# Full attention begun at the tenth projection step, weight loads in pieces and their squares one group ahead

## The chip, the cores and the metric

The kernel runs on one core of one Trainium2 chip. The metric is device time in microseconds (us), the median of several runs. The engines have short names here: PE (TensorE, matrix products), ACT (ScalarE, activations), DVE (VectorE), POOL (GpSimd), SP (the queue that issues most DMAs).

## What is computed

One layer of a bidirectional encoder over 1024 tokens of width 1024, batch 1, float32. Two groups of heads read one combined projection of the normalised input.

```python
h = _rmsnorm(x, norm_gain[l])
proj = h @ w_in[l]                                  # 1024 x 3328 columns
q_a, k_a, v_a, g_a, q_b, k_b, v_b, g_b = jnp.split(proj, split_at, axis=-1)
q_a = rotary(_rmsnorm(q_a, q_norm_a)); k_a = rotary(_rmsnorm(k_a, k_norm_a))
o_a = _gqa_blocked(q_a, k_a, v_a) * silu(g_a)       # 8 query heads, 2 key heads, full attention
o_b = _neighbourhood_attn(q_b, k_b, v_b, na_rpb) * silu(g_b)   # 8 heads, window 8 x 16 of the token grid
x = x + jnp.concatenate([o_a, o_b], -1) @ w_out[l]
return _rmsnorm(x, final_norm_gain)
```

## The kernel before

Every float32 operand is split into a float16 high part and a float16 remainder, and each product is three matmuls (high x high, high x low, low x high). The 1024 tokens are eight tiles of 128. The weights come as 17 groups of 256 columns, 1 MB each: 0 is keys and values of the full attention (KVA), 1 and 2 its queries (QA), 3 and 4 the queries, 5 and 6 the keys, 7 and 8 the values of the neighbourhood attention (QB, KB, VB), 9 and 10 its gate, 11 and 12 the gate of the full attention, 13 to 16 the output projection. A projection of a group is four "pairs" of two token tiles, 48 matmuls of 128x256 each.

A group's weights are prepared before use. `load_w(g)` has POOL issue the DMA into one of two buffers `raw`. `prep_a` (L281) squares the whole group on ACT and sums by row; the output of the squares, which nobody reads, goes into the group's own future buffer `whl`, of which there are two. `prep_b` sums over the partitions with one small matmul (L293), then DVE (L294) and POOL's power (L295) make the scale. `prep_c` (L300) casts the high part on ACT in two halves, `prep_d` (L307) forms the remainder on DVE. `prep(g)` is called when group g-1 begins and sets the slots of these steps; `PREP` holds delays for single groups; `load_w(g + 2)` comes after the casts.

The order is made in two ways. PE's instructions run in the order in which the program writes them. ACT, DVE, POOL and SP are, after a short opening, ordered by the framework's planner from its own simulated times, with the program's order as the priority. The program itself is written by a small class, `Flow`: it counts slots; `at(delay, position, function)` puts work into a later slot; `queue` holds generators whose every `yield` stands for six projection matmuls (three of 128x512 for KB); `step(n)` runs one slot and then takes n yields from the queue.

First come 12 steps of 8 yields (`fl.step(PAIR)`): groups 0, 1 and 2, a pair a step. Every pair of keys or queries is normalised and rotated (`norm_rope`, L411 to L429, on ACT, DVE and POOL) and transposed by DMA (L447, L480). Then `run_units` goes through 64 units of full attention, one head of one tile each, the four heads of the first query group for all tiles first. A unit is `a_qk` (scores of 128x1024 into one of two PSUM buffers, L592 to L594; a pass of DVE, L601; two exponentials on ACT, L603 and L604), `a_lo` one slot later (remainder on DVE, L609, and a DMA transpose of the probabilities, L614) and `a_pv` (product with the values, L623 to L625) four slots later. Between units PE takes yields of the queue, groups 3 to 8, at a rate of `FILL_A`: 4.2 for four units, 3.4 for seven, then 2.65.

The same follows for 64 units of the neighbourhood attention (`b_qk`, `b_lo`, `b_pv`, L673 to L705, transposes at L692, values five slots later) with the rates `FILL_B` and `FILL_B_END` and groups 9 to 16 in the queue. `SPLIT_AT` names the unit after which each finished tile of the gated output is normalised, split and transposed (`os_a`, `os_b`, `os_c`, L731 to L748). Groups 13 to 16 are used for tiles 0 to 3 two at a time; `out_row(u)` then does one later tile through all four groups, 16 yields, adds to the input (L772), applies the final norm (L796 to L805) and stores (L806). Row 4 is in the queue with the units; rows 5, 6 and 7 come after the last unit.

Of the kernel before, what the change touches and what calls it, by code (L numbers as in the profile page):

```python
# [16 lines left out]
P = 128  # L17
KC = 8
NU = 8
GC = 256  # L20
NH = 8
D = 64
NX = 4
SKEW_A, SKEW_B = 4, 5
FILL_A = [(4, 4.2), (7, 3.4)]
FILL_A_END = 3
FILL_B = [(12, 3.4), (24, 3), (2, 2.5)]
FILL_B_END = 3
SPLIT_AT = (26, 27, 29, 31, 39, 55, 56)
PREP = {2: 4, 3: 0, 4: 2, 12: 0, 13: 0}  # L30
NEG = -1.0e38
EPS = 1e-6
LN_P = 14.0 * float(np.log(2.0))
# [5 lines left out]
KVA, QA, QB, KB, VB, GA, GB = 0, 1, 3, 5, 7, 11, 9  # L39
# [3 lines left out]
class Flow:  # L43
# [8 lines left out]
    def at(self, delay, pos, fn, *a):  # L52
        self.due.setdefault((self.slot + delay, pos), []).append((fn, a))
# [35 lines left out]
def kernel(ctx: ExitStack, tc: tile.TileContext, x: bass.AP, w: bass.AP, wo: bass.AP,  # L89
# [3 lines left out]
    act, dve, pool, pe, sp = nc.scalar, nc.vector, nc.gpsimd, nc.tensor, nc.sync  # L93
# [9 lines left out]
    fl = Flow()  # L103
    at = fl.at
# [46 lines left out]


    raw, wp, late, x2 = {}, {}, {}, {}

    def load_w(g):
        raw[g] = wraw.tile([P, KC, GC], F32, tag="raw", name=f"raw{g}")
        if g in gate:
            pool.tensor_copy(raw[g][:, 0, :1], xr[gate[g]][:, 1:])
        pool.dma_start(raw[g], w[g] if g < 13 else wo[g - 13])

    xts, gate = [], {}
    ones = area(0, [P], F32)[:1]
# [3 lines left out]
    mh = one.tile([P, NU], F32, name="mh")  # L166
# [25 lines left out]
    S_, RC, EC = 0, 17, 34  # L192
# [5 lines left out]
    def col(i, n=1):  # L198
        return sm[:, i:i + n]
# [68 lines left out]

    wss = {}

    def prep_a(g):
# [7 lines left out]
        wss[g] = tn(f"wss{g}", 1, "ws")  # L279
        if g:  # L280
            act.activation(wp[g][0].bitcast(BF16), raw[g], AF.Square, accum_out=wss[g])  # L281
            return
        late["half"] = tn("wssh", 1, "ws")
        act.activation(wp[g][0][:, :4].bitcast(BF16), raw[g][:, :4], AF.Square, accum_out=late["half"])

    def prep_a2(g):
        dve.tensor_tensor_reduce(out=wp[g][0][:, 4:].bitcast(BF16), in0=raw[g][:, 4:], in1=raw[g][:, 4:], scale=1.0,
                                 scalar=late["half"], op0=OP.mult, op1=OP.add, accum_out=wss[g])

    def prep_b(g):  # L290
        pt = ahead.append(proj_tile(f"wt{g}")) or ahead[-1]
        top = [a.bitcast(BF16)[:, 1:2] for a in (mh[:, :1], wss[g])]
        pe.matmul(pt[:, 0, :1], top[0].to_broadcast([P, P]), top[1], start=True, stop=True)  # L293
        dve.tensor_scalar(wss[g], pt[:, 0, :1], -2.0 ** -27, 1e-30, op0=OP.mult, op1=OP.add)  # L294
        pool.tensor_tensor(col(S_ + g), wss[g], mh[:, :1], op=OP.pow)  # L295

    def prep_c(g):
        for i in range(0, KC, KC // 2):
            s = slice(i, i + KC // 2)
            act.activation(wp[g][0][:, s], raw[g][:, s], AF.Copy, scale=col(S_ + g))  # L300

    def prep_d(g):
        ready.add(g)
        n = KC if g == 0 else KC // 2
        for i in range(0, KC, n):
            s = slice(i, i + n)
            dve.scalar_tensor_tensor(wp[g][1][:, s], raw[g][:, s], col(S_ + g), wp[g][0][:, s], op0=OP.mult, op1=OP.subtract)  # L307
# [8 lines left out]
    ready = set()  # L316

    def prep_e(g):
        dve.reciprocal(col(RC + g), col(S_ + g))
# [13 lines left out]

    pend = []

    def prep(g):
        d = PREP.get(g, 1)
        at(d + 1, "pre", prep_a, g)
        at(d + 2, "mid", pend.append, g)

    def sums_now():

        while pend:
            g = pend.pop(0)
            prep_b(g)
            at(1, "pre", prep_c, g)
            at(1, "post", prep_d, g)
            if g + 2 < 17:
                at(2, "pre", load_w, g + 2)

    def fin_scales():
        for hh in range(2):
# [39 lines left out]
        return hT[a][:, k, u * P:(u + 1) * P]  # L392

    kTa = r6(0, [P, NU, 3, P], F16, "kTa")
    va = r6(1, [P, NU, 2, 2, D], F16, "va")
    qTa = [carve(rq, 8192 * i, [NU, 4, P], F16) for i in range(2)]
    klo1 = carve(rq, 16384, [NU, P], F16)

    def norm_rope(g, up, src, nh, kq, done):
        n = 2 * nh  # L400
        s3 = src.rearrange("p a (h d) -> p a h d", d=D)
        if g == KVA:
            both = slot("both", [P, 2, 2, nh, D], F32)
        else:
            both = w4((0, 1, 8, 9)[up] if g == QA + 1 else 4 + up, [P, 2, 2, nh, D], F32, f"qn{g}_{up}")
        qn, t2 = both[:, 0], both[:, 1]
        sq = t2
# [24 lines left out]
        at(1, "mid", b)  # L432
        at(1, "post", c)
        done(qn)
# [375 lines left out]
    PAIR = 8.0  # L810
# [28 lines left out]
    k, q = [kva_gen(up) for up in UP], group(1, [qa_gen(0, up) for up in UP])  # L839
# [34 lines left out]
    x_lo(7, dve)  # L874
    load_w(3)

    for p in range(11):
        fl.step(PAIR)
    fl.add(*group(3, [qb_gen(0, up) for up in UP]))
    fl.add(*group(4, [qb_gen(1, up) for up in UP]))  # L880
# [57 lines left out]
    def out_row(u):  # L938
        last = ([out_gen([(u, 15), (u, 16)], [(u, 1)])] if u < NU - 1 else
                [out_gen([(u, 15)]), out_gen([(u, 16)], [(u, 1)])])  # L940
        return out_gen([(u, 13), (u, 14)], [(u, 0)]), *last
# [101 lines left out]
```

## Time and profile before

| | |
|---|---|
| median of 3 runs | 609.66 us (609.57 to 610.23) |
| the profiled execution | 611.81 us, its span 610.0 us |
| mean granted PE clock | 0.967 |
| PE busy | 534.4 us, 88% of the span |
| DVE, ACT, POOL busy | 440.6, 394.9, 119.3 us |
| DMA queue 1 (transposes and SP's loads) | 67.7% of 16 engines' span |

Busy time is read by stage, since each stage has another limit: a busy share over the whole span mixes them. The profile names an instruction by its line, its engine and its output and inputs; in the timeline a bracket behind an instruction gives the time that its engine had stood idle before it, and what ended that. A DMA has a time to landing, from its issue to its end. The chain of waits follows the work that ended last, back from the end.

### The profile page before, as it was taken

The page shows a single profiled execution, that of the slowest core. Times are in us where ns is not written, and L with a number is a line of the kernel's source. Part 1 is how long each engine was busy: PE and PEld are TensorE (multiplying, and loading weights), DVE is VectorE, ACT ScalarE, POOL GpSimd, SP SyncE. Part 2 cuts the span into 40 slices and gives each one's busy share as a digit, 9 for nine tenths or more (in the row PEclk, how much of TensorE's full clock was granted, in tenths as well). Part 3 has the DMA queues.
Part 4 walks back from the last instruction along what each step waited for, and adds up shares of the span by engine and source line. Part 5 has one row for each costly group of instructions (what it writes and reads, how often), then busy time and mean ns, then how long its engine had stood idle before and what let it go on. Part 6 is the DMA issues. An engine that isn't in the chain of part 4 may idle for free.

```text
span 610.0 us, 13863 instructions
## 1 busy us (share of the span) xinstructions
PE 534.4 (88%) x5541; PEld 405.4 (66%) x5541; DVE 440.6 (72%) x986; ACT 394.9 (65%) x647; POOL 119.3 (20%) x150
## 2 busy tenths in 40 slices
PE   3587989799988979979888979999999789889794
PEld 1376878577864535547666767877777567668684
DVE  4688676987977948957977847586877866778332
ACT  5552454878859858858667727677689986674210
POOL 2396788410000000000000000110111221112100
PEclk9978999999999979989899999999999898999899
DMA  8989433799999999999799894548486996687422
GB/s 231 225 160 247 96 105 106 136 213 195 204 198 168 197 173 169 206 207 187 155 183 210 155 217 122 118 76 134 103 149 122 172 212 145 134 140 183 95 62 70
DMA packets 245972, 97.26 MB, mean 159 GB/s; under 512 B 236561, under 2 KB 237201, under 8 KB 243986
## 3 DMA queue, kind: packets, MB, share of 16 engines
q1 hardware_dynamic: 242306, 75.66, 67.7%
q0 software_dynamic: 3312, 19.92, 11.6%
q10 hardware_dynamic: 288, 0.79, 0.5%
q8 instruction: 43, 0.70, 0.5%
q14 instruction: 23, 0.19, 0.1%
HBM read 31.33 MB, written 4.19 MB: 58 GB/s over the span
## 4 chain that ended last, share of the span: by engine, by line
PE 44%; DMA 14%; issue 14%; DVE 13%; POOL 6%; ACT 5%; SPq 1%; DVEq 0%; POOLq 0%; ACTq 0%
PE pj L369 14%; PE wt L369 7%; DMA ar<-p 6%; PE po L369 5%; PE kb L369 4%; DMA ar<-ar 4%; PE s L592 3%; PE s L594 2%; POOL nt L417 2%; PE sb L674 2%; DVE whl L307 2%; ACT p L604 2%; DVE p L601 1%; PE sb L673 1%; ACT p L603 1%
## 5 line engine op out<-in xcount | busy, mean ns | idle before, releaser
L369 PEld LDWEIGHTS <-hT 128*128 128x128 f16 x2112 | 205.6, 100 | 68.5 <-issue 15.4
L369 PE MATMUL pj<-whl,hT 128*128 128x256 f16 x1584 | 189.2, 275 | 3.4 <-DMA hT<-xhl 1.8
L601 DVE CUSTOM_DVE_ANT_0 p<-s,sm 128x1024 f32<-128x1024 f32 x64 | 82.0, 1281 | 15.4 <-PE s L594 13.9
L603 ACT ACTIVATE p<-s,nm,sm 128x1024 f16<-128x1024 f32 x43 | 51.8, 1204 | 51.1 <-DMA ar<-p 23.4
L369 PE MATMUL wt<-whl,hT 128*128 128x256 f16 x528 | 68.0, 286 | 14.9 <-ACT whl L300 7.1
L604 ACT ACTIVATE p<-s,nm,sm 128x1024 f32<-128x1024 f32 x64 | 76.8, 1200 | 0.0
L609 DVE TENSOR_TENSOR p<-p,p 128x1024 f16<-128x1024 f32 x43 | 52.8, 1229 | 21.7 <-ACT p L604 21.6
L369 PE MATMUL po<-whl,mA 128*128 128x256 f16 x384 | 65.8, 277 | 0.0
L684 ACT ACTIVATE rq<-ar,mx,sm 128x384 f32<-128x384 f32 (+1 forms) x64 | 43.0, 673 | 28.6 <-DVE mx L683 28.4
L295 POOL TENSOR_TENSOR sm<-wss,mh 128x1 f32<-128x1 f32 x17 | 11.0, 645 | 250.1 <-DVE wss L294 237.4
L369 PEld LDWEIGHTS <-mA 128*128 128x128 f16 x512 | 48.7, 100 | 12.3 <-issue 5.0
L369 PE MATMUL po<-whl,mB 128*128 128x256 f16 x192 | 53.1, 277 | 0.0
L592 PE MATMUL s<-kTa,rq 128*128 128x512 f16 x128 | 39.5, 391 | 14.6 <-ACT p L604 14.6
L623 PE MATMUL pv<-va,ar 128*128 128x64 f16 x384 | 39.3, 194 | 8.7 <-DMA ar<-p 7.4
L307 DVE SCALAR_TENSOR_TENSOR whl<-raw,sm,whl 128x1024 f16<-128x1024 f32 (+1 forms) x33 | 44.8, 1371 | 1.9 <-ACT whl L300 1.9
L685 ACT ACTIVATE ar<-ar,mx,sm 128x384 f16<-128x384 f32 (+1 forms) x64 | 42.9, 674 | 1.1
L623 PEld LDWEIGHTS <-ar 128*128 128x128 f16 x384 | 34.7, 99 | 13.1 <-DMA ar<-p 9.3
L300 ACT ACTIVATE whl<-raw,sm 128x1024 f16<-128x1024 f32 x34 | 37.1, 1138 | 5.0 <-POOL sm L295 4.9
L681 DVE CUSTOM_DVE_ANT_0 ar<-sb,bias 128x384 f32<-128x384 f32 x48 | 26.6, 555 | 18.4 <-PE sb L674 15.4
L625 PE MATMUL pv<-va,ar 128*128 128x64 f16 x384 | 39.3, 194 | 0.0
L624 PE MATMUL pv<-va,ar 128*128 128x64 f16 x384 | 39.3, 194 | 0.0
L690 DVE TENSOR_TENSOR ar<-rq,ar 128x384 f16<-128x384 f32 (+1 forms) x64 | 34.1, 533 | 4.8 <-ACT ar L685 4.8
(196 smaller groups left out, 1069.3 us busy)
## 6 DMA issues: line engine op xcount, KB each, us to landing
raw<-in_w_dram POOLq DMA_DIRECT2D x11, 1024.0 KB, 6.7
raw<-in_wo_dram POOLq DMA_DIRECT2D x4, 1024.0 KB, 5.9
x<-in_x_dram SPq DMA_DIRECT2D x7, 512.0 KB, 6.4
khh<-ar SPq DMA_DIRECT2D x16, 128.0 KB, 3.7
x2b<-in_x_dram POOLq DMA_DIRECT2D x4, 512.0 KB, 5.9
x<-in_x_dram POOLq DMA_DIRECT2D x4, 512.0 KB, 6.8
out_dram<-x2b SPq DMA_DIRECT2D x8, 256.0 KB, 3.0
out_dram<-x SPq DMA_DIRECT2D x7, 256.0 KB, 2.9
```

Of the source, the lines that this page charges most:

```text
L307: dve.scalar_tensor_tensor(wp[g][1][:, s], raw[g][:, s], col(S_ + g), wp[g][0][:, s], op0=OP.mult, op1=OP.subtract)
L369: pe.matmul(*o[0], **o[1])
L592: pe.matmul(s[:, c * 512:(c + 1) * 512], q, kTa[:, 4 * c:4 * c + 4, hh], start=True, stop=False)
L601: dve.tensor_tensor_reduce(out=p32, in0=s, in1=col(SHA).to_broadcast([P, 1024]), scale=col(NSA), scalar=3e38, op0=OP.add, op1=OP.min, accu ...
L603: act.activation(hl[:, 0], s, AF.Exp, bias=nm, scale=col(SCA))
L604: act.activation(p32, s, AF.Exp, bias=nm, scale=col(SCA), accum_out=sums[hh, u][:, h:h + 1])
L609: dve.tensor_tensor(hl[:, 1], p32, hl[:, 0], op=OP.subtract)
L623: pe.matmul(o, pt[:, kt], va[:, kt, hh, 0], start=kt == 0, stop=False)
L624: pe.matmul(o, pt[:, kt], va[:, kt, hh, 1], start=False, stop=False)
L625: pe.matmul(o, pt[:, 8 + kt], va[:, kt, hh, 0], start=False, stop=kt == 7)
L684: act.activation(p32, t, AF.Exp, bias=mx, scale=col(SCB + hh), accum_out=sums["b", u][:, h:h + 1])
L685: act.activation(hl[:, 0], t, AF.Exp, bias=mx, scale=col(SCB + hh))
```

## The change

1. The plain projection steps are 9 instead of 12, so full attention begins at the tenth. The last three pairs of group 2 (24 yields) stay in the queue and go between the units; the later rate of `FILL_A` rises from 2.65 to 3.10 yields a unit. The normalisation of group 2 takes two staging areas in turn instead of four, as two of the old ones belong to the units now.
2. Loads of groups 6 to 16 are issued in four pieces of 256 KB, one a slot.
3. For these groups the squares are taken a group ahead, as four ACT instructions of 128x512 with four sums, into a spare area; `prep_b` adds the four sums with four small matmuls. When group g-1 begins, g's cast and remainder follow at once, half a group in each of two slots.
4. `PREP`: group 2 is prepared one step earlier; 12 and 13 have no delay of their own.
5. `FILL_B` and `FILL_B_END` become 3.35 yields for 40 units and 3.1 after. Rows 5 and 6 join row 4 in the queue; by the rates row 5 is done between the units, and row 6 stands between the last tile's `os_b` and `os_c`. `SPLIT_AT` has the tiles 5 and 6 at units 47 and 55 instead of 55 and 56.

```diff
-FILL_B = [(12, 3.4), (24, 3), (2, 2.5)]
-FILL_B_END = 3
-SPLIT_AT = (26, 27, 29, 31, 39, 55, 56)
-PREP = {2: 4, 3: 0, 4: 2, 12: 0, 13: 0}
+FILL_B = [(40, 3.35)]
+FILL_B_END = 3.1
+SPLIT_AT = (26, 27, 29, 31, 39, 47, 55)
+PREP = {2: 3, 3: 0, 4: 2}
...
-        pool.dma_start(raw[g], w[g] if g < 13 else wo[g - 13])
+        src = w[g] if g < 13 else wo[g - 13]
+        if g < 6:
+            pool.dma_start(raw[g], src)
+            return
+        for i in range(4):
+            k = slice(2 * i, 2 * i + 2)
+            issue = lambda k=k: pool.dma_start(raw[g][:, k], src[:, k])
+            at(i, "pre", issue) if i else issue()
...
+    def prep_q(g, i):
+        junk = (va_more if g < 11 else carve(rq, 17408, [512], BF16)).rearrange("p (k c) -> p k c", c=GC)
+        if i == 0:
+            wss[g] = [t[:, 0:1] for t in [tn(f"wss{g}_{k}", 1, "ws") for k in range(4)]]
+        act.activation(junk, raw[g][:, 2 * i:2 * i + 2], AF.Square, accum_out=wss[g][i])
...
-        pe.matmul(pt[:, 0, :1], top[0].to_broadcast([P, P]), top[1], start=True, stop=True)
-        dve.tensor_scalar(wss[g], pt[:, 0, :1], -2.0 ** -27, 1e-30, op0=OP.mult, op1=OP.add)
-        pool.tensor_tensor(col(S_ + g), wss[g], mh[:, :1], op=OP.pow)
+        n = len(wss[g])
+        for i in range(n):
+            pe.matmul(pt[:, 0, :1], top[0].to_broadcast([P, P]), top[1 + i], start=i == 0, stop=i == n - 1)
+        t = wss[g][0]
+        dve.tensor_scalar(t, pt[:, 0, :1], -2.0 ** -27, 1e-30, op0=OP.mult, op1=OP.add)
+        pool.tensor_tensor(col(S_ + g), t, mh[:, :1], op=OP.pow)
...
+    def squares(g, slots):
+        for i, k in enumerate(slots):
+            at(k, "pre", prep_q, g, i)
+        at(slots[-1], "mid", pend.append, g)
+
     def prep(g):
-        d = PREP.get(g, 1)
-        at(d + 1, "pre", prep_a, g)
-        at(d + 2, "mid", pend.append, g)
+        if g < 6:
+            d = PREP.get(g, 1)
+            at(d + 1, "pre", prep_a, g)
+            at(d + 2, "mid", pend.append, g)
+            if g == 5:
+                squares(g + 1, (7, 7, 8, 8))
+            return
+        at(1, "pre", alloc_wp, g)
+        for i, h in enumerate(HALVES):
+            at(1 + i, "pre", prep_c, g, [h])
+            at(1 + i, "post", prep_d, g, [h])
+        if g + 2 < 17:
+            at(3, "pre", load_w, g + 2)
+        if g < 16:
+            squares(g + 1, (4, 5, 6, 7) if g < 13 else (2, 2, 3, 3))
...
-            both = w4((0, 1, 8, 9)[up] if g == QA + 1 else 4 + up, [P, 2, 2, nh, D], F32, f"qn{g}_{up}")
+            both = w4(8 + up % 2 if g == QA + 1 else 4 + up, [P, 2, 2, nh, D], F32, f"qn{g}_{up}")
...
-    for p in range(11):
+    for p in range(8):
         fl.step(PAIR)
...
-    mid = (6 * 32 - sum(n * r for n, r in FILL_A) - FILL_A_END * SKEW_A) / (64 - n_head) + 0.02
+    mid = (6 * 32 + 24 - sum(n * r for n, r in FILL_A) - FILL_A_END * SKEW_A) / (64 - n_head) + 0.02
...
-    fl.add(*out_row(4))
+    fl.add(*out_row(4), *out_row(5), *out_row(6))
...
-    for u in range(5, NU):
-        fl.add(*out_row(u))
-        while fl.queue:
-            fl.step(PAIR)
+    fl.add(*out_row(7))
+    while fl.queue:
+        fl.step(PAIR)
```

More of the change, by code (lines that the diff above doesn't have):

```diff
@@ L269, with alloc_wp @@
     wss = {}
-    def prep_a(g):
+    def alloc_wp(g):
         if g < 15:
@@ L278, in prep_a @@
         wp[g] = (t[:, 0], t[:, 1])
-        wss[g] = tn(f"wss{g}", 1, "ws")
+    def prep_a(g):
+        alloc_wp(g)
+        wss[g] = [tn(f"wss{g}", 1, "ws")]
         if g:
-            act.activation(wp[g][0].bitcast(BF16), raw[g], AF.Square, accum_out=wss[g])
+            act.activation(wp[g][0].bitcast(BF16), raw[g], AF.Square, accum_out=wss[g][0])
             return
@@ L284, in prep_a @@
         act.activation(wp[g][0][:, :4].bitcast(BF16), raw[g][:, :4], AF.Square, accum_out=late["half"])
+    def prep_q(g, i):
[3 more added lines that the diff above has]
+        act.activation(junk, raw[g][:, 2 * i:2 * i + 2], AF.Square, accum_out=wss[g][i])
     def prep_a2(g):
         dve.tensor_tensor_reduce(out=wp[g][0][:, 4:].bitcast(BF16), in0=raw[g][:, 4:], in1=raw[g][:, 4:], scale=1.0,
-                                 scalar=late["half"], op0=OP.mult, op1=OP.add, accum_out=wss[g])
+                                 scalar=late["half"], op0=OP.mult, op1=OP.add, accum_out=wss[g][0])
@@ L290, in prep_b @@
     def prep_b(g):
         pt = ahead.append(proj_tile(f"wt{g}")) or ahead[-1]
-        top = [a.bitcast(BF16)[:, 1:2] for a in (mh[:, :1], wss[g])]
-        pe.matmul(pt[:, 0, :1], top[0].to_broadcast([P, P]), top[1], start=True, stop=True)
-        dve.tensor_scalar(wss[g], pt[:, 0, :1], -2.0 ** -27, 1e-30, op0=OP.mult, op1=OP.add)
-        pool.tensor_tensor(col(S_ + g), wss[g], mh[:, :1], op=OP.pow)
[L297 to L300, printed above, removed]
@@ L302, in prep_d @@
-    def prep_d(g):
+        top = [a.bitcast(BF16)[:, 1:2] for a in (mh[:, :1], *wss[g])]
+        n = len(wss[g])
[4 more added lines that the diff above has]
+        pool.tensor_tensor(col(S_ + g), t, mh[:, :1], op=OP.pow)
+        scaled.add(g)
+    HALVES = [slice(i, i + KC // 2) for i in range(0, KC, KC // 2)]
@@ L303, in prep_d, with prep_c @@
+    def prep_c(g, halves=HALVES):
+        assert g in scaled
+        for s in halves:
+            act.activation(wp[g][0][:, s], raw[g][:, s], AF.Copy, scale=col(S_ + g))
+    def prep_d(g, halves=HALVES):
+        for s in halves if g else [slice(0, KC)]:
+            dve.scalar_tensor_tensor(wp[g][1][:, s], raw[g][:, s], col(S_ + g), wp[g][0][:, s], op0=OP.mult, op1=OP.subtract)
+        if halves[-1] != HALVES[-1]:
+            return
         ready.add(g)
-        n = KC if g == 0 else KC // 2
@@ L305, in prep_d @@
-        for i in range(0, KC, n):
-            s = slice(i, i + n)
-            dve.scalar_tensor_tensor(wp[g][1][:, s], raw[g][:, s], col(S_ + g), wp[g][0][:, s], op0=OP.mult, op1=OP.subtract)
         if g > 1:
@@ L314, in prep_d @@
                 load_x2(2 * g - 26 + i)
-    ready = set()
+    ready, scaled = set(), set()
     def prep_e(g):
@@ L334 @@
     pend = []
+    def squares(g, slots):
+        for i, k in enumerate(slots):
+            at(k, "pre", prep_q, g, i)
+        at(slots[-1], "mid", pend.append, g)
     def prep(g):
-        d = PREP.get(g, 1)
-        at(d + 1, "pre", prep_a, g)
-        at(d + 2, "mid", pend.append, g)
+        if g < 6:
[4 more added lines that the diff above has]
+                squares(g + 1, (7, 7, 8, 8))
+            return
+        at(1, "pre", alloc_wp, g)
[6 more added lines that the diff above has]
+            squares(g + 1, (4, 5, 6, 7) if g < 13 else (2, 2, 3, 3))
     def sums_now():
@@ L345, in sums_now @@
             prep_b(g)
+            if g > 5:
+                continue
             at(1, "pre", prep_c, g)
             at(1, "post", prep_d, g)
-            if g + 2 < 17:
-                at(2, "pre", load_w, g + 2)
+            at(2, "pre", load_w, g + 2)
     def fin_scales():
@@ L394 @@
     kTa = r6(0, [P, NU, 3, P], F16, "kTa")
-    va = r6(1, [P, NU, 2, 2, D], F16, "va")
+    va_all = r6(1, [P, 3072], F16, "va")
+    va = va_all[:, :2048].rearrange("p (u h e d) -> p u h e d", u=NU, h=2, e=2)
+    va_more = va_all[:, 2048:2560].bitcast(BF16)
     qTa = [carve(rq, 8192 * i, [NU, 4, P], F16) for i in range(2)]
```

## The prediction

> **What bounds the kernel now.** I read the page first, then busy time by stage, then what TensorE (PE) waited for. Stages follow the program: projection groups 0 to 2 alone (40 to 101 us), full attention with groups 3 to 8 between its units (101 to 366), neighbourhood attention with groups 9 to 12 and the output projection (366 to 570), last output rows (570 to 610).
>
> ```profile
> span 610.0 us, 13863 instructions
> ```
>
> ```profile
> core 0: us, PE busy (x) PEld busy (x) DVE busy (x) ACT busy (x) POOL busy (x), PEclk, DMA share, GB/s
> ...
> 40.00:101.00 61.00, 55.09 (x486) 47.59 (x484) 46.43 (x81) 27.91 (x48) 47.89 (x51) 0.97 0.57 128
> 101.00:366.00 265.00, 236.38 (x2754) 166.42 (x2752) 207.50 (x347) 190.09 (x253) 18.98 (x22) 0.97 0.99 187
> 366.00:570.00 204.00, 190.94 (x1934) 150.79 (x1930) 147.64 (x469) 149.28 (x301) 31.06 (x49) 0.98 0.70 139
> 570.00:610.00 40.00, 32.01 (x280) 27.83 (x278) 14.02 (x35) 6.40 (x16) 2.87 (x6) 0.93 0.26 67
> ```
>
> The second column is PE busy. In the projection stage PE is nearly full and the DMA engines are little used; in full attention PE idles 265 - 236.4 = 28.6 us while the DMA share stands at 0.99; in the third stage it idles 13.1 us. So full attention is the only long stage in which PE has room, and what holds it must be something else. The tile view of the scores s gives its pace, the source view of the probabilities' transposes (L614) their landing:
>
> ```profile
> L592 PE MATMUL s<-kTa,rq x128: 376/379/634, 100.9 to 349.1; 128*128 128x512 f16 x128
> ...
> L601 DVE CUSTOM_DVE_ANT_0 p<-s,sm x64: 1272/1283/1285, 105.9 to 351.4; 128x1024 f32<-128x1024 f32 x64
> ```
>
> ```profile
> DMA to landing us min/median/max: 4.2/4.6/9.3
> ```
>
> 64 units, from 100.9 to 349.1 us in 63 steps: 3.94 us each. PE's own share of that is about 236.4 / 265 x 3.94 = 3.51 us. A transpose lands in 4.6 us as a rule, 9.3 at worst. The worst one is found in the chain that ended last, with the weight load that POOL issued just before it, and with what PE then waited for (timeline, POOL and PE):
>
> ```profile
> 207.95 9.32 DMA ar<-p
> ```
>
> ```profile
> 205.59 0.57 POOL L159 DMA_DIRECT2D raw<-in_w_dram  x1 [5.04 <-DVE whl L307]
> ```
>
> ```profile
> 217.32 0.20 PE L623 MATMUL pv<-va,ar 128*128 128x64 f16 x1 [2.47 <-DMA ar<-p]
> 219.80 1.01 PE L592 MATMUL s<-kTa,rq 128*128 128x512 f16 x2 [1.53 <-ACT p L604]
> ```
>
> A load of 1 MB at 205.6 doubles the landing of the transpose behind it; PE loses 2.47 us on it and 1.53 us on the scores' buffer that ACT gives back late: 4.0 us.
>
> **The change part by part.**
>
> *Attention begins three projection steps earlier.* A yield is six matmuls; their price, from the chain of waits:
>
> ```profile
> 129.45 1.97 PE wt L369 x18
> ```
>
> 18 in 1.97 us, so a yield is 0.657 us and the 24 yields that move from the projection stage into attention are 15.8 us. Nothing is taken off PE: they are gained if they fit into the idle time there, lost if attention grows by as much. With 15.8 us over 64 units and 4 of drain, PE's need rises from 3.51 to 3.74 us a unit, still under the 3.94 that the units take. So I take attention's length as unchanged at 265 us: its idle falls from 28.6 to 12.8 us. Bounds: the idle stays whole (+15.8 us) or goes wholly (236.4 + 15.8 = 252.2, so -12.8 us). Are its inputs there three steps earlier, some 18 us? The first score, the tile view of kTa and its landings:
>
> ```profile
> 100.95 0.38 PE L592 MATMUL s<-kTa,rq 128*128 128x512 f16 x1
> ```
>
> ```profile
> L480 SPq DMA_TRANSPOSE kTa<-ar x4: 1212/1227/1464, 55.9 to 76.1; - x4
> ...
> DMA to landing us min/median/max: 2.7/2.8/3.6
> ```
>
> The last keys are issued at 76.1 and land by 79.7; the first score would come near 82.7. Three microseconds of margin, so yes. What the early units share instead: three normalisations of the second query group with POOL (47.9 of 61 us busy in that stage) and DVE. Their evacuation off PSUM is ACT's alone, so PE is not held by POOL; the two staging areas that replace four hold the third query step until the first is copied out. The units waited here before also (first score 100.9, first DVE pass 105.9). I put it at nothing; it is inside the bounds above.
>
> *Group 2's weights one step earlier.* Before, PE stood at the first step of group 2 (timeline, PE):
>
> ```profile
> 78.17 0.27 PE L369 MATMUL wt<-whl,hT 128*128 128x256 f16 x1 [0.99 <-ACT whl L300]
> 79.58 1.47 PE L369 MATMUL wt<-whl,hT 128*128 128x256 f16 x12 [1.14 <-DVE whl L307]
> 81.39 3.98 PE L369 MATMUL wt<-whl,hT 128*128 128x256 f16 x35 [0.33 <-DVE whl L307]
> ```
>
> 2.5 us. A step is 5.3 us, so with the sums one step earlier the wait goes: -2.5 us (bounds -2.5 and 0).
>
> *Squares a group ahead, weights cast as their group begins.* From group 6 the order sum, power, cast no longer runs inside the group before. In the third stage PE stood at the first use of groups 13 to 16 (timeline, PE):
>
> ```profile
> 483.21 0.27 PE L369 MATMUL wt<-whl,mA 128*128 128x256 f16 x1 [1.86 <-ACT whl L300]
> 484.54 0.37 PE L369 MATMUL wt<-whl,mA 128*128 128x256 f16 x1 [1.05 <-DVE whl L307]
> ...
> 503.79 0.27 PE L369 MATMUL wt<-whl,mA 128*128 128x256 f16 x1 [2.42 <-DVE whl L307]
> ...
> 520.98 0.27 PE L369 MATMUL wt<-whl,mA 128*128 128x256 f16 x1 [0.98 <-DVE whl L307]
> ...
> 539.04 0.27 PE L369 MATMUL wt<-whl,mA 128*128 128x256 f16 x1 [1.69 <-DVE whl L307]
> ```
>
> 1.86 + 1.05 + 2.42 + 0.98 + 1.69 = 8.0 us. The casts now start one slot after the previous group's start, more than four slots before use, so I take -8.0 us (bounds -8.0 and 0). The granted clock in the same stretches:
>
> ```profile
> 480.00:500.00 20.00, 17.09 (x162) 13.06 (x161) 13.71 (x49) 16.63 (x31) 6.00 (x12) 0.91 0.88 204
> 500.00:520.00 20.00, 17.57 (x169) 13.14 (x167) 13.08 (x41) 15.35 (x29) 2.37 (x4) 0.91 0.73 156
> ```
>
> 0.09 of 20 us is 1.8 us in each, 3.6 us together, not in my sum; it is an end of the range. The Trainium skill, "TensorE: Matmul & The Clock Gate", section on the HAM clock gate, says that an idle window of about 3.4 us halves PE's clock until it has been busy again; by that rule the clock comes back with the stalls and the sum ends 3.6 us lower. The trace agrees in part: the clock is low where the stalls are, though the one of 2.42 us is shorter than the page's window.
>
> What this costs: ACT's square of a whole group against four pieces, by the source views of L281 and of a 128x512 square, L796:
>
> ```profile
> L281 ACT ACTIVATE whl<-raw x16: 1894/1908/1925, 16.6 to 511.7; 128x2048 bf16<-128x2048 f32 x16
> L281 ACT ACTIVATION_READ_ACCUMULATOR whl<-raw x16: 186/192/216, 18.4 to 513.5; 128x1 f32 x16
> ```
>
> ```profile
> L796 ACT ACTIVATE ar<-x x8: 629/630/631, 562.3 to 602.6; 128x512 bf16<-128x512 f32 x8
> ```
>
> 4 x 0.63 - 1.91 + 3 x 0.19 = 1.2 us a group, 13 us over 11 groups, beside ACT's idle time (75 us in full attention, 55 in the third stage): nothing. Without that cover the exponentials come late and PE waits for the scores' buffer. Casts and remainders are as before in number and size. PE gets three more one-column matmuls a group, 33 in all; such a one and its follower start 0.03 us apart (timeline, PE):
>
> ```profile
> 74.37 0.17 PE L293 MATMUL wt<-wss,mh 128*128 128x1 bf16 x1
> 74.40 2.78 PE L369 MATMUL pj<-whl,hT 128*128 128x256 f16 x24
> ```
>
> +1.0 us (bounds 1.0, and 33 x 0.17 = 5.6 if none overlapped).
>
> *Loads in four pieces.* POOL issues four instead of one, 0.57 us each by the row at 205.59: 1.7 us more for 11 groups, on an engine busy 19 of 265 us. Behind a piece stand POOL's power and gate products, which PE doesn't meet directly: nothing. What the pieces change for the transposes is unknown; I count no gain for them beyond the length held above, which is where the fewer late transposes would pay.
>
> *Rows 5 and 6 between units.* By the rates, 40 x 3.35 + 29 x 3.1 = 223.9 yields against 210.8 run between units; the third stage grows by 13 x 0.657 = 8.6 us of dense PE work and the tail shrinks by the same: zero. But the tail loses cover. The last tile's values (timeline, PE), its two transposes (timeline, SP) and their landing (L748):
>
> ```profile
> 568.71 0.19 PE L705 MATMUL sb<-ar 128*128 128x64 f16 x1
> ```
>
> ```profile
> 577.45 1.98 SPq L748 DMA_TRANSPOSE mA<-mhl  x1
> 579.53 1.25 SPq L748 DMA_TRANSPOSE mB<-mhl  x1
> ```
>
> ```profile
> DMA to landing us min/median/max: 3.1/3.3/3.5
> ```
>
> 579.5 + 3.5 - 568.7 = 14.3 us. Rows 5 and 6 covered it (32 yields, 21 us); now row 6 alone does, 16 yields or 10.5 us. So PE waits 3.8 us before row 7; bounds 0, if the planner hurries the chain, and 3.8. I take 3.8, as the row has it.
>
> **Sum:** -15.8 - 2.5 - 8.0 + 1.0 + 3.8 = -21.5 us. The profiled execution took 611.81 us with its 610.0 us span, so it would take 590.3; the median of the runs is 609.66, 2.15 lower, so 588 us.
>
> **The rivals.**
> *Attention is full already.* The idle of 28.6 us is latency, not room: each load still delays the transposes by as much, and the 15.8 us add up. Then 588 + 15.8 = 604 us. For it: loads and transposes share engines at a share of 0.99. Against: 3.74 is under 3.94. The Trainium skill, "DMA: Bandwidth & Descriptors", section on queues, rings and completion order, says each engine takes turns between queues packet by packet; by that rule the bytes of the pieces delay the transposes as the whole did. The trace agrees as far as 9.32 us against 4.6 goes.
> *Attention's idle goes too.* Pieces and a fuller PE hide the stalls, length 252 to 258 us: 575 to 581 us.
> *A new wait at the weights.* Groups 15 and 16: the last piece is issued three slots after the first, and their sums stand in PE's order; if squares are late, PE waits there instead. The 8.0 us stay: 596 us.
> *Slower: the pieces spread the stall.* Each piece catches another unit's transpose and costs PE what the whole load did, 4.0 us. Five loads of groups 6 to 10 in attention make 20 pieces: 20 x 4.0 against 5 x 4.0, +60 us, 648 us. It decides from (21.5 + 20) / 20 = 2.1 us a piece. Against it: a piece has a quarter of the bytes, and values are used four units, some 15 us, after the scores.
>
> **How the numbers follow.** Forecast 0.43, 588 us (own range 581 to 596); attention's idle goes 0.18; attention full 0.16; new wait 0.12; pieces spread the stall 0.07; parts cancel out, within 0.2%, 0.04. From 0.2% on a measurement of this kernel can tell a change. Faster: 0.43 + 0.18 + 0.16 + 0.12 = 0.89; same 0.04; slower 0.07. The range takes in the first four: 573 (575 less part of the clock's 3.6) to 604.
>
> **What would show it.** First score near 83 us instead of 100.9; units 3.9 us apart over 64; PE idle in full attention near 13 us; no wait for whl of over 1 us at the first use of groups 13 to 16; last row of the transposes' landing well under 9.3; a wait of 0 to 4 us ahead of row 7. The prediction is wrong if units take 4.2 us or more, if early units wait for the query normalisations, or if PE stands at the sums.

## The result, and the profile after

The changed kernel took 634.06 us (median of four runs, 632.72 to 635.05), the kernel before, run beside it, 609.62: a ratio of 1.0417, 95% interval 1.0361 to 1.0474. Ratios, here and below, leave out the runs that lie more than 1.5% above the quickest run of their kernel, and are not quotients of the medians. The forecast was 588 us with a range of 573 to 604. The profiled execution took 634.15 us.

The windows of the changed kernel, cut where its stages begin: first score to first neighbourhood score, from there to the last product with the neighbourhood values, and the rest. The columns are as in the prediction.

```profile
core 0: us, PE busy (x) PEld busy (x) DVE busy (x) ACT busy (x) POOL busy (x), PEclk, DMA share, GB/s
83.80:379.70 295.90, 256.33 (x2921) 183.40 (x2919) 222.80 (x372) 204.32 (x303) 44.90 (x55) 0.94 0.96 170
379.70:601.30 221.60, 199.86 (x2022) 159.30 (x2019) 148.35 (x466) 150.21 (x331) 40.87 (x63) 0.96 0.71 131
601.30:632.30 31.00, 22.19 (x205) 19.19 (x202) 12.16 (x32) 5.56 (x14) 2.92 (x5) 0.96 0.34 69
```

The same windows of the kernel before:

```profile
100.90:366.20 265.30, 236.68 (x2761) 166.71 (x2759) 207.60 (x347) 190.29 (x254) 19.09 (x22) 0.97 0.99 186
366.20:568.70 202.50, 189.44 (x1916) 149.50 (x1913) 147.00 (x466) 149.08 (x301) 30.51 (x48) 0.98 0.70 140
568.70:610.00 41.30, 33.31 (x294) 28.91 (x291) 14.66 (x38) 6.40 (x16) 3.42 (x6) 0.92 0.26 65
```

The first score comes 17.1 us earlier and the tail is 10.3 us shorter, but attention is 30.6 us longer and the third stage 19.1: together 22.3 us slower, the difference of the spans. PE busy in attention rose by 19.7 us: the 15.8 us that were moved there, and some 4 us more at a granted clock of 0.94 instead of 0.97. PE's idle time rose as well, from 28.6 to 39.6 us. In the third stage idle time rose from 13.1 to 21.7 us. The pace of the units (tile view of the scores) and the landing of the probabilities' transposes (source view of their line):

```profile
L635 PE MATMUL s<-kTa,rq x128: 376/379/634, 83.8 to 365.6; 128*128 128x512 f16 x128
```

```profile
DMA to landing us min/median/max: 4.2/4.8/14.5
```

(365.6 - 83.8) / 63 = 4.47 us a unit against 3.94. The median landing hardly moved; the worst one rose from 9.3 to 14.5 us. One place of this kind is seen from five sides: the four pieces of a load on POOL (timeline), SP's transposes (timeline), the chain of waits (with the row of another such place above it), and the gaps of ACT and PE (timelines; in brackets the idle time and what ended it):

```profile
342.25 2.17 POOL L165 DMA_DIRECT2D raw<-in_w_dram  x4 [13.79 <-DVE whl L327]
```

```profile
343.15 14.23 SPq L657 DMA_TRANSPOSE ar<-p  x2
```

```profile
204.51 14.48 DMA ar<-ar
...
343.15 14.84 DMA ar<-p
```

```profile
358.07 1.21 ACT L646 ACTIVATE p<-s,nm,sm 128x1024 f16<-128x1024 f32 x1 [11.12 <-DMA ar<-p]
```

```profile
358.03 0.24 PE L666 MATMUL pv<-va,ar 128*128 128x64 f16 x1 [6.96 <-DMA ar<-p]
```

The pieces, which the program puts into four slots, leave POOL back to back in 2.17 us: a slot is a priority for the planner, not a time, and POOL had nothing else to do. Two transposes that SP issues beside them occupy SP for 14.23 us, and by the chain the first of them, issued at 343.15, has landed only 14.84 us later. (The landing view holds only the transposes whose landing the profile can tell; this one is not among them.) PE waits 6.96 us for the transposed probabilities, ACT 11.12 us for a buffer. In this stretch the DMA engines pass for busy throughout, yet move less than the stage's 170 GB/s:

```profile
340.00:362.00 22.00, 12.99 (x142) 9.66 (x142) 11.58 (x18) 10.08 (x14) 2.17 (x4) 0.80 1.01 133
```

The granted clock is 0.80 here. Most loads pass without this. Of the six in attention two are caught, those issued at 203.6 and 342.3 us: their slowest piece landed after 12.2 and 13.9 us, that of the other four after 5.1 to 8.8 (source view of the pieces, load by load). PE's waits by what ended them (total, times, longest), those on DMAs that were absent or smaller before:

```profile
PE pv L666 <- DMA ar<-p: 9.7, 3, 7.0
PE po L410 <- DMA mB<-mhl: 8.4, 2, 8.0
...
PE pvb L746 <- DMA ar<-ar: 6.3, 3, 4.2
...
PE pv L666 <- DMA ar<-ar: 5.4, 1, 5.4
...
PE po L410 <- DMA mA<-mhl: 3.1, 2, 2.7
```

Before, PE's waits on such transposes were these:

```profile
PE pv L623 <- DMA ar<-p: 7.4, 4, 2.5
...
PE sb L703 <- DMA ar<-ar: 4.3, 3, 2.0
...
PE pv L623 <- DMA ar<-ar: 1.2, 1, 1.2
```

In the third stage it is again loads on POOL's queue, here pieces and the x2 rows, beside transposes on SP's (timeline, POOL; chain of waits):

```profile
505.82 2.21 POOL L165 DMA_DIRECT2D raw<-in_wo_dram  x4 [5.89 <-DVE whl L327]
...
511.30 1.10 POOL L806 DMA_DIRECT2D x2b<-in_x_dram  x2
```

```profile
511.07 12.21 DMA mB<-mhl
```

### The profile page after: what moved, and what is told of

It reads as the page before. It is cut to its first block, busy times and chain, and to the rows that moved or that the text cites. A ratio compares the mean times of both kernels' runs of the same rounds, so it can differ in the third digit from the quotient of the medians.

```text
span 632.3 us, 14092 instructions
## 1 busy us (share of the span) xinstructions
PE 537.1 (85%) x5574; PEld 408.2 (65%) x5574; DVE 442.8 (70%) x986; ACT 402.0 (64%) x713; POOL 138.1 (22%) x183
## 4 chain that ended last, share of the span: by engine, by line
PE 39%; DMA 22%; DVE 14%; issue 13%; ACT 6%; POOL 3%; SPq 1%; DVEq 0%; POOLq 0%; ACTq 0%
PE pj L410 15%; DMA ar<-ar 8%; PE po L410 6%; PE wt L410 5%; DMA ar<-p 4%; DMA mB<-mhl 3%; DVE p L644 2%; PE s L635 2%; PE kb L410 2%; DVE p L652 2%; ACT p L647 2%; PE s L637 2%; PE sb L717 2%; DMA x2b<-in_x_dram 2%; DMA hT<-xhl 1%
## 5 line engine op out<-in xcount | busy, mean ns | idle before, releaser
L410 PEld LDWEIGHTS <-hT 128*128 128x128 f16 x2112 | 207.2, 100 | 67.9 <-DMA hT<-xhl 14.5
L410 PE MATMUL pj<-whl,hT 128*128 128x256 f16 x1584 | 192.3, 278 | 3.1 <-DVE va L505 1.9
L410 PE MATMUL wt<-whl,hT 128*128 128x256 f16 x528 | 66.6, 282 | 13.4 <-DMA hT<-xhl 6.9
L646 ACT ACTIVATE p<-s,nm,sm 128x1024 f16<-128x1024 f32 x43 | 51.8, 1206 | 38.2 <-DMA ar<-p 20.3
L410 PE MATMUL po<-whl,mA 128*128 128x256 f16 x416 | 71.6, 277 | 3.1 <-DMA mA<-mhl 3.1
L410 PE MATMUL po<-whl,mB 128*128 128x256 f16 x208 | 57.5, 277 | 8.4 <-DMA mB<-mhl 8.4
L315 POOL TENSOR_TENSOR sm<-wss,mh 128x1 f32<-128x1 f32 x17 | 10.9, 643 | 208.8 <-DVE wss L314 201.1
L666 PE MATMUL pv<-va,ar 128*128 128x64 f16 x384 | 40.3, 196 | 15.0 <-DMA ar<-p 9.7
L646 ACT ACTIVATE ar<-s,nm,sm 128x1024 f16<-128x1024 f32 x21 | 25.4, 1207 | 29.8 <-DVE nm L644 19.9
L668 PE MATMUL pv<-va,ar 128*128 128x64 f16 x384 | 40.3, 196 | 0.0
L667 PE MATMUL pv<-va,ar 128*128 128x64 f16 x384 | 40.3, 196 | 0.0
```

What stands on the lines that cost most here:

```text
L410: pe.matmul(*o[0], **o[1])
L646: act.activation(hl[:, 0], s, AF.Exp, bias=nm, scale=col(SCA))
L666: pe.matmul(o, pt[:, kt], va[:, kt, hh, 0], start=kt == 0, stop=False)
L667: pe.matmul(o, pt[:, kt], va[:, kt, hh, 1], start=False, stop=False)
L668: pe.matmul(o, pt[:, 8 + kt], va[:, kt, hh, 0], start=False, stop=kt == 7)
```

## The experiments

Theory: a load on POOL's queue and the transposes on SP's queue can slow each other far down; four pieces make that likelier, and attention pays. Rivals: attention is full and the moved yields lengthen it; the squares on ACT do it; the rows between units do it. A time is the median of all runs; "before" is the kernel before, run beside it.

**1. Loads whole.** In `load_w` the loop over pieces becomes one `pool.dma_start(raw[g], src)`; all else as changed.

> The changed kernel with the weight loads whole again (1 MB in one DMA), all else as changed. Theory 1, the pieces slow the transposes: a load goes back from 14.8 us to about 9 us of landing for the transpose behind it, the waits of PE after loads in full attention fall from some 37 us to 16 us, those on transposes in the third stage from 20 us to under 8 us: 595 to 606 us. Theory 2, the earlier attention and the higher fill crowd the DMA engines whatever the loads look like: 625 to 635 us.

615.83 us (before 609.06). The four runs lie in two pairs, at 610.5 and 611.8 and at 619.9 and 621.3 us. The pieces cost 18 us of the 24 by the median, 23 by the quicker pair. The rest of the change isn't the gain forecast either, and the 595 to 606 us of the first theory were missed: whole loads on POOL's queue still meet the transposes at times (last section).

**2. Pieces alone.** The kernel before with

```
for i in range(4):
    pool.dma_start(raw[g][:, 2*i:2*i+2], src[:, 2*i:2*i+2])   # g >= 6, in slots i
```

> The kernel before with the loads of groups 6 to 16 in the same four pieces, nothing else. Theory 1: 15 to 25 us slower than before, 625 to 635 us, and transposes that land 12 us or more after their issue. Theory 2: as before, 608 to 612 us.

621.31 us, ratio 1.0207 (1.0163 to 1.0252). The landing of the probabilities' transposes:

```profile
DMA to landing us min/median/max: 4.2/4.6/16.1
```

The pieces do harm without anything else of the change: 12 us, a little less than the 15 to 25 expected.

**3. Pieces cut by partitions.** `raw[g][32*i:32*i+32], src[32*i:32*i+32]` on the changed kernel.

> The changed kernel with its four pieces cut by partitions (32 partitions of 8 KB each) instead of by columns (128 partitions of 2 KB each): as many DMAs, but packets as long as those of a whole load. Theory 1 in the form that the number and size of packets costs: 600 to 612 us. In the form that four DMAs cost, whatever their packets: 628 to 636 us. Theory 2: 628 to 636 us.

641.59 us, 1.0541 (1.0485 to 1.0596): worse than by columns, though each piece now has stretches of 8 KB instead of 2. The short stretches of the column cut are not what does the harm.

**4. The early start alone.** The kernel before with `range(8)` in place of `range(11)`, 24 yields more in `mid`, and the staging areas of the change.

> The kernel before with attention begun at the tenth step and the rate of 3.10 alone; loads whole, weights prepared as before, output rows as before. Theory 1: the 15.8 us of projection fit into attention's idle time, 593 to 600 us. Theory 2: attention grows by as much or more than it starts earlier, 608 to 625 us.

609.56 us (603.03 to 615.25), 0.9971 (0.9924 to 1.0017). Not distinguishable from no change, with a wide spread.

**5. The kernel before with its loads on SP's queue.** `(pool if g < 4 else sp).dma_start(raw[g], ...)`.

> The kernel before with the whole loads of groups 4 to 16 issued on SP's queue, the one of the transposes, instead of POOL's. Theory 1 in its sharper form (a load on POOL's queue that is still in flight when SP issues the second transpose behind it makes both crawl; 11 to 17 us for 1 MB instead of 4 to 5): with one queue there is nothing to take turns, loads take 3 to 4 us, PE's idle time in full attention falls from 28 to 15 us or less: 592 to 603 us. Rival, a load costs the transposes its bytes whatever the queue: 606 to 613 us; or SP stands at the loads' wait for a free buffer and the transposes behind it come late: over 615 us.

606.94 us, 0.9949 (0.9922 to 0.9976): 3 us, just inside what the rival by bytes gave and not the 592 to 603 of the theory. Whole loads of the kernel before cost little on POOL's queue.

**6. Whole loads of the changed kernel on SP's queue.** Experiment 1 with the same line.

> The changed kernel with whole loads (as in the first of these experiments) on SP's queue from group 4 on. Theory 1: no load crawls, 585 to 600 us. Rival, bytes: 610 to 618 us. Rival, SP stands at the loads: over 620 us.

604.82 us, against 615.83 with these loads on POOL's queue. The four runs are 594.6, 604.3, 605.3 and 608.4 us, so this gives the direction and no price; neither the 585 to 600 of the theory nor the rivals' times were met. The x2 rows were still loaded by POOL here.

**7. The pieces on SP's queue.** The changed kernel with `sp.dma_start` for the pieces and the whole loads from group 4 on.

> The changed kernel with its four pieces, issued on SP's queue. Theory 1, two queues that take turns are needed for the crawl: 585 to 603 us. If four DMAs of 2 KB rows are slow in themselves: 620 to 635 us.

600.84 us, 0.9839 (0.981 to 0.9869). The same pieces, cut the same way, are 33 us cheaper on the other queue. So the cut isn't dear by itself; it is dear on POOL's queue, beside SP's transposes. One wait of this kind was left, with the x2 rows still loaded by POOL:

```profile
PE po L410 <- DMA mB<-mhl: 6.8, 2, 6.4
```

**8. Pieces on POOL's queue, one a unit.** Ahead of the second to fourth piece POOL copies one column, the row maximum of the unit just before, into the piece's buffer, so that a piece can't leave before that unit.

> The changed kernel with the second to fourth piece held back on POOL until the row maximum of the unit before that slot is there (a copy of one column into the piece's place), so that a piece is issued a unit instead of four in 2.2 us. Theory 1: a piece takes about 1.5 us and is over before the second transpose comes, no crawl, 590 to 606 us. Rival, every piece beside transposes costs as it does now: 630 to 645 us.

617.63 us, 1.0125 (1.0076 to 1.0175): 16 us better than back to back, 17 worse than on SP's queue. The pieces of a load left 1.1 to 13.6 us apart. Spreading them takes away half of the harm.

**9. The x2 rows on SP's queue too.** Experiment 7 with `sp.dma_start(x2[u], ...)`.

> The changed kernel with its pieces, and the loads of groups 4 and 5, on SP's queue measured 600.8 us, and one long wait was left in its second stage: 6.8 us of PE for the transposed mhl beside the x2 loads, the last big ones on POOL's queue. Here those go to SP's queue too. If that wait is a load on one queue beside transposes on the other, it goes: 594 us (592 to 597). If the transposes of mhl are merely issued late by their own chain, the time stays at 600 to 601. If SP, which issues in order, now stands at an x2 load until the last reader of the old tile is done and holds the transposes behind it, 603 or more.

595.93 us, 0.978 (0.9731 to 0.983). The wait for mB went with it, and this is the whole change with nothing but the queue altered, 38 us below it:

```profile
PE po L410 <- DMA mB<-mhl: 1.8, 2, 1.3
```

```profile
82.90:359.80 276.90, 249.13 (x2920) 181.20 (x2918) 222.49 (x372) 204.45 (x302) 31.37 (x30) 0.99 0.97 182
359.80:563.70 203.90, 197.23 (x2026) 158.82 (x2023) 150.53 (x466) 150.03 (x331) 23.31 (x35) 0.99 0.70 142
563.70:594.20 30.50, 22.06 (x204) 19.12 (x199) 12.16 (x32) 5.56 (x14) 2.93 (x5) 0.93 0.35 69
```

Attention is 19.0 us shorter than in the changed kernel, the third stage 17.7; the granted clock is 0.99 in both. The distance between the pieces isn't all of it: in this run, too, SP issued all four pieces of some loads back to back (timeline, SP). Probabilities' transposes land in 8.2 us at worst:

```profile
173.10 2.00 SPq L165 DMA_DIRECT2D raw<-in_w_dram  x4
```

```profile
DMA to landing us min/median/max: 4.3/4.8/8.2
```

**10. The early start without the interference.** Experiments 4 and 5 together.

> The kernel before with two edits: attention begins at the tenth projection step as in the change, and the weight loads from group 4 on stand on SP's queue. With the second edit alone it measured 606.9 us, with the first alone 609.6. If the early start was hidden only by loads that disturb the transposes, its full 15.8 us show once they are gone: 591 us. If attention is full, so that the 24 yields lengthen it by what they take, the time stays at 605 to 608. What the traces of the two single edits give (the first score 15.3 us earlier, attention 5.8 us longer than before) lies between: about 598.

596.98 us, 0.9793 (0.9746 to 0.984): 10 us below experiment 5, not the 15.8 of the forecast, not nothing. Attention in experiment 5 and here:

```profile
103.00:363.60 260.60, 235.11 (x2761) 167.19 (x2759) 207.29 (x347) 190.46 (x254) 14.60 (x15) 0.97 1.03 190
```

```profile
85.20:351.50 266.30, 246.02 (x2906) 179.39 (x2903) 218.47 (x363) 196.66 (x264) 30.73 (x26) 0.99 1.02 189
```

It starts 17.8 us earlier and is 5.7 us longer: PE busy grows by 10.9 us, at a granted clock of 0.99 instead of 0.97, and idle time falls from 25.5 to 20.3 us, by 5.2 and not by 15.8.

**11. The rows of the kernel before, x2 by POOL.** Experiment 7 with `FILL_B`, `FILL_B_END`, `SPLIT_AT` and the three rows behind the last unit as before.

> The changed kernel with its loads on SP's queue (600.8 us), with the second stage's rows and rates of the kernel before: one output row between units, three behind them. This prices the rows alone. The tail was 22.3 us with the change's rows and 31.4 to 33.0 without, the second stage 209.5 us with them and 202.1 to 206.3 without: the rows should be worth 2 to 7 us, so 603 to 608 here. If the second stage is full, they only change places: 600 to 602. If the rows between units cost more than they save, below 599.

615.94 us, 1.012 (1.0067 to 1.0173), 15 us slower, more than any theory gave. PE's waits:

```profile
PE sb L746 <- DMA ar<-ar: 12.8, 3, 5.8
PE pvb L746 <- DMA ar<-ar: 7.5, 2, 6.5
```

Other transposes now stood beside the x2 loads of POOL, so this does not price the rows alone. The next experiment has the same rows without these loads on POOL's queue, and is 13 us quicker.

**12. The same rows, all loads on SP's queue.**

> The change with all its loads on SP's queue (595.9 us), with the second stage's rows and rates of the kernel before: one output row between units, three behind them. The earlier run of this edit still had the x2 loads on POOL's queue, beside the transposes of units that the changed rows had run sooner. From the last score to the end it is 249.8 us with the change's rows, and 258.5 in the kernel before with the early start and its loads on SP: the rows should be worth 8.7 us, so 604.6 (601 to 607). If that run's 615.9 was the price of the rows themselves, 609 to 612. If they are worth nothing, 595 to 597.

602.96 us, 0.99 (0.9868 to 0.9932): 7 us above experiment 9 and within the range expected. Its third stage and its tail:

```profile
361.80:562.60 200.80, 187.39 (x1933) 148.49 (x1929) 146.95 (x460) 148.51 (x329) 22.69 (x34) 1.00 0.71 141
562.60:604.30 41.70, 32.91 (x294) 28.79 (x291) 14.66 (x38) 6.39 (x16) 3.44 (x6) 0.91 0.24 64
```

The change's rows lengthen the third stage by 203.9 - 200.8 = 3.1 us and shorten the tail by 11.2.

**13. Two halves of 512 KB on POOL's queue.** `range(2)` and `slice(4*i, 4*i+4)`.

> The change with each weight load in two halves of 512 KB instead of four pieces of 256 KB, on POOL's queue as in the change (whole loads measured 615.8 us, four pieces 634.1). If each further DMA stretches the load beside the transposes, so that more loads are still in flight when the next transpose is issued, the time lies between: 620 to 628. If any cut does the whole harm, 632 to 636; if only small pieces do, 614 to 618.

613.75 us (607.42 to 621.5), 1.0051 (1.0021 to 1.0081): not to be told from whole loads. The harm doesn't grow evenly with the number of pieces; it comes between two and four.

**14. No squares ahead.** Experiment 9 with the sum, scale and cast of all groups inside the group before, as in the kernel before.

> The change with all its loads on SP's queue (595.9 us), its squares, scale and cast again inside their own group as in the kernel before; pieces, early attention and rows stay. With the loads out of the way the first to the last score still take 261.1 us, against 249.2 in the kernel before with the early start alone and its loads on SP. If the squares a group ahead make those 11.9 us (they stand on ScalarE among the exponentials), attention is 249 to 251 here, the waits for the weights of groups 13 to 16 come back (8.0 us by the prediction), and the time is 592 (588 to 596). If the pieces make them, on SP's queue too, attention stays at 261 and the waits come back on top: 602 to 606.

592.77 us, 0.9716 (0.9681 to 0.9751); experiment 9 had 0.978 (0.9731 to 0.983). Attention and third stage:

```profile
83.10:354.50 271.40, 247.03 (x2906) 179.95 (x2904) 221.10 (x366) 197.27 (x265) 31.84 (x29) 0.99 1.00 185
354.50:561.30 206.80, 196.52 (x2007) 157.94 (x2004) 147.77 (x472) 150.59 (x303) 23.52 (x36) 0.99 0.72 140
```

Without the squares ahead attention is 5.5 us shorter and the third stage 2.9 longer. The intervals overlap; that they are worth 8 us is excluded, that they cost some 3 is likely. The expected 592 us was hit with luck: both the 11.9 us taken off and the 8.0 us put back turned out smaller.

**15. Squares ahead for groups 13 to 16 alone.**

> As the one with no squares ahead, but with the squares a group ahead for the last four groups (13 to 16) alone, none of which stands in the first stage. If the squares lengthen attention where they stand in it, and pay only at groups 13 to 16, this takes the gain without the price: 595.9 - 11.9 = 584 (581 to 588). If the pieces lengthen attention, 594 to 598. If the squares ahead are worth nothing at the last four groups either, the same as with none ahead.

592.39 us, 0.9737 (0.9706 to 0.9768): the 584 of the theory failed. At the last groups, too, the squares ahead give nothing that can be told apart.

**16. Experiment 14 with whole loads.**

> As the one with no squares ahead, but with whole loads in place of the pieces: the kernel before with attention begun early, the rows of the change and all loads from group 4 on SP's queue. If the pieces are free on SP's queue, it equals the one with pieces within 2 us. If they cost attention there too, it is 5 us or more faster than that one, with the first to the last score in 249 us against 255 or more.

594.06 us, 0.9756 (0.9717 to 0.9795). On SP's queue pieces and whole loads are equal.

**17. The pieces on a queue of ACT.** Experiment 9 with `act.dma_start` for the pieces.

> The change with all its loads on SP's queue (595.9 us), but with the pieces issued by ScalarE, on a queue of its own beside SP's transposes. If any load on a second queue can collapse together with the transposes, some loads take over 9 us here as they did on POOL's queue (11.9 and 13.2 us in the change), and the time is 610 to 630. If that belongs to POOL's queue, all loads take under 7 us and the time is 594 to 602, with what ScalarE stands at the issues as the difference.

607.78 us (602.89 to 614.98), 0.9958 (0.9921 to 0.9994), between the two theories' values and 12 us above SP's queue. Landing of the pieces, and of the probabilities' transposes:

```profile
DMA to landing us min/median/max: 3.0/5.0/11.1
```

```profile
DMA to landing us min/median/max: 4.2/4.9/11.9
```

On SP's queue (experiment 9) the worst piece took 7.4 us and the worst transpose 8.2. So slow landings come with this second queue too, while POOL's is the dearer one. How much of the 12 us they are is open: the 44 issues alone take 22 us of ACT (timeline, added up), which in experiment 9 SP does.

## Why the prediction was wrong

**The step that failed** is the pair of "I take attention's length as unchanged at 265 us" and, for the pieces, "What the pieces change for the transposes is unknown; I count no gain". An unknown of either sign was put at zero without a row for it, and a loss was left out of the range. By windows attention grew by 30.6 us; PE's idle time there, which was to fall by 15.8 us, rose by 11.0. Experiment 1 shows 18 to 23 of the 24 us of the whole loss as the price of the pieces, experiments 7 and 9 that it is paid only with loads on POOL's queue. Why two queues can come down together is not shown.

**The rival on the other side** had the place and the sign: "the pieces spread the stall", 648 us, with a chance of 0.07. It was wrong in the mechanism. Pieces do not each cost a unit 4 us; most loads pass. The rows show single encounters of a load and transposes at 203.6, 342.3 and 505.8 us, with waits of PE of 5.4, 7.0 and 8.0 us behind them. The rival's count was off as well: the loads of six groups, 6 to 11, stand in attention, in both kernels, and not of five. The row at 205.59 us in the profile before (landing 9.32 us) was the worst of its trace, and I used it as the usual price of a load. It doesn't even price the load: SP had issued three copies of 128 KB just ahead of that transpose, and with the weight loads on SP's queue the worst landing is still 9.1 us (experiment 10). The argument against the rival, that values are used some 15 us after the scores, failed because one transpose with another behind it took 14.84 us.

**Early attention, -15.8 us.** The first score came at 83.8 us, as said. Without the weight loads on POOL's queue the early start is worth 10 us (experiments 5 and 10): attention grew by 5.7 us where it was held to be unchanged, so "attention is full already" is a third true. With the loads on POOL's queue the gain isn't measurable (experiment 4). The forecast's own falsifier, units of 4.2 us or more, came true with 4.47.

**Squares ahead, -8.0 us.** The five waits at groups 13 to 16 went, but their removal paid nothing: in experiment 9 against 14 the third stage is 2.9 us shorter, and attention pays 5.5. What I put at "nothing" on ACT is visible there in its source view of the squares (idle time of ACT ahead of them, us and times, experiment 9):

```profile
  DMA raw<-in_w_dram: 12.5, 8
  DMA raw<-in_wo_dram: 6.1, 6
```

ACT stands at the squares until a piece lands; 10.3 us of this, in 7 waits, lie in attention (the same view in that window). That this is what lengthens attention is argued from these rows; the runs show only that attention is longer with the squares ahead.

**Rows, 8.6 - 8.6 + 3.8 us.** The sign was wrong: the rows are worth 7 us (experiment 12). The third stage grew by 3.1 us and not 8.6: between experiments 12 and 9 PE busy there rises by 9.8 us and its idle time falls from 13.4 to 6.7, room that the prediction had read as 13.1 us and did not use. The wait ahead of row 7 is 0.45 + 0.42 us, not 3.8 (timeline, PE, changed kernel):

```profile
613.12 0.39 PE L410 MATMUL po<-whl,mA 128*128 128x256 f16 x2 [0.45 <-DMA mA<-mhl]
...
613.94 0.27 PE L410 MATMUL po<-whl,mB 128*128 128x256 f16 x1 [0.42 <-DMA mB<-mhl]
```

**Group 2, -2.5 us.** With this edit the first score comes at 82.7 to 83.2 us in twelve of fourteen profiles (83.8 and 84.3 in the others), without it at 85.2 and 85.7 (experiments 10 and 4): 2 to 3 us. How much of that reaches the end was not timed alone. The 1.0 us for small matmuls was not tested.

**The clock.** The granted clock was 0.94 in attention and not higher than before. It was low where the stalls were, 0.80 in the row at 340 us, and 0.99 in experiment 9 without them.

With all loads on SP's queue the changed kernel does gain, 12.6 us on the kernel before (608.5 to 595.9, experiment 9), and 15.3 without the squares ahead (608.1 to 592.8, experiment 14, with the 592.4 and 594.1 of the next two not to be told from it). Some 3 us of that are the queue's own, by the kernel before (experiment 5), so 9 to 12 us of the forecast's 21.5 were there, about half; it was the queue of the loads that turned the sign. The parts do not add up: the rows are worth 7 us beside the squares ahead, yet from experiment 10 to experiment 14, which has the rows and the earlier weights of group 2 on top, the time falls by 4.2.

## What to carry to other kernels

When a change cuts or moves transfers that run beside others on another queue, and no row of the trace prices that, put a loss into the range and not only zero. The worst landing of the trace before is a place to start from, but not the price: here it was 9.3 us, and still 9.1 with the weight loads on the other queue. Try loads that must run beside transposes on the transposes' own queue first; here cutting them was free there. A slot or a priority in a program isn't a time: read off the timeline whether pieces are spread at all before counting on it.

## What the runs showed of the hardware

Loads of 1 MB on POOL's queue and DMA transposes on SP's usually share: in the kernel before, PE's longest wait for a transpose of probabilities or of outputs was 2.5 us. At times both come down together: 14.84 us for one transpose, with a second behind it, beside four pieces in the changed kernel, with 133 GB/s moved at a DMA share of 1.01. With the loads from group 4 on and the x2 rows on SP's queue (experiments 9, 12, 14, 15 and 16) that wait was 2.0 to 2.8 us at most, in the changed kernel 8.0. The Trainium skill, "DMA: Bandwidth & Descriptors", section on queues, rings and completion order, says that each DMA engine goes round the queues that it has work for, one packet at a time. The traces agree only in so far as both second queues that were tried have slow landings (experiment 17: 11.9 us at worst) and the one shared queue has a lower worst (experiment 9: 8.2); the fall in bytes moved does not follow from that rule. What tips a load into it is left open: not the shape of the cut (experiment 3), and not the cut alone (experiment 13). The profile lists POOL's queue as software_dynamic, SP's and ACT's as hardware_dynamic; whether POOL's is the dearer one for that reason, no run shows. Spreading the pieces helps (experiment 8), and single whole loads are caught too, as in experiment 1 (source view of the loads; PE's waits), where PE stood 13.0 us at one transpose behind the load issued at 143.1 us:

```profile
DMA to landing us min/median/max: 5.5/6.0/19.5
```

```profile
PE pv L660 <- DMA ar<-p: 13.5, 2, 13.0
```
